# A float32 network of three layers on one core: weight tiles and dense-layer activation tiles at multiples of 64 bytes in SBUF

## The chip, the cores and the metric

The kernel runs on one core of one Trainium2 chip. The metric is the time of the device in microseconds, the median of several executions. A core has five engines with queues of their own: TensorE (PE, with its weight loads shown apart as PEld), VectorE (DVE), ScalarE (ACT), GpSimd (POOL) and SyncE (SP). Its working memory, SBUF, has 128 partitions; an address below is a number of bytes within a partition, the same in all of them.

## The reference

One sequence of 256 tokens with 1024 features goes through a stack of layers in float32. Cut to its frame:

```python
# first block, twice: half-FFN, mixer, half-FFN; the mixers are a sparse attention with
# a short convolution, and then a delta-rule recurrence (RWKV-7) over 16 heads of 64
h = rmsnorm(x, pre_g); h = (silu(h @ w_gate) * (h @ w_up)) @ w_down
x = x + 0.5 * rmsnorm(h, post_g)
x = x + rmsnorm(mixer(rmsnorm(x, g), ...), g_post)
# second block: FFN, a state-space branch beside an attention to the 64 best keys,
# attention to a memory of 256 tokens, FFN; each with layer_norm(ALPHA * x + f(x))
# third block, with 16 tokens in front: FFN, gated linear attention, FFN, FFN,
# windowed attention over shared keys and values, FFN
```

Each FFN has 1024 x 2816 weights for gate and up and 2816 x 1024 for down. Nearly all the arithmetic is in these dense products, `x @ w` for 256 or 272 tokens.

## The kernel before

Activations lie feature-major: a tile [128, k, tokens] holds features on the partitions and tokens along them. Weights are read once from DRAM, in pieces of [128, 1024] float32, 512 KB each. `Mat.load` (L198) starts the DMA into one of six `raw` tiles on SP's queue. `Mat.get` (L216) then parts each piece in two: ScalarE copies it to a float32r tile `wh` (L230), VectorE subtracts that from `raw` and writes the rest to `wl` (L231). There are five tiles of each, used in turn. Activations are parted in the same way into `xh` and `xl` (`split_x`, L254: L263 on ScalarE, L264 on VectorE), `hh` and `hl`, and so on.

A dense product is then three float32r matmuls that add up in PSUM, in `mm3p` (L531):

```python
        t.matmul(out, wh, xh, start=first, stop=False, **kw)    # L534
        t.matmul(out, wh, xl, start=False, stop=False, **kw)    # L535
        t.matmul(out, wl, xh, start=False, stop=last, **kw)     # L536
```

The first operand is stationary: 128 columns of weights, loaded into the array for each matmul. The second moves: 256 or 272 columns of tokens, 1024 or 1088 bytes of a partition. In `proj_tok_steps` (L458 to L460) it is the other way round: weights move, activations are stationary.

The program is one long list of such products with the norms, softmaxes and recurrences between them. A planner doesn't exist; the order of each engine is the order in which the Python emits instructions. `ffn` (L462) does, for each of 11 blocks of 256 columns, all products of gate and of up, and then `out_proj` (L555) the down projection, 22 parts of the contraction for each of four pairs of output tiles. In the mixers, `stagger` and `weave` alternate steps of attention or recurrence with steps of dense products.

Where tiles lie. SBUF is allotted in the order in which pools and tiles are asked for, each tile rounded up to a multiple of 32 bytes. From the left: small constants, `vec` at 16512, `zero`, the table `tab_all` at 18944 (`tables`, L826, through `load_tables`: the arrays `ident`, `ones`, `inv_d` and `causal` side by side, one transfer), and then `raw`, `wh`, `wl`, `x`, `tmp`, `tiny`; from 136480 on the pools of each phase. `tab_all` has 128 + 1 + 128 + 384 = 641 columns, 2564 bytes, rounded to 2592. In the built program that leads to these starts:

| tiles | start | mod 64 |
|---|---|---|
| raw (6), wh (5), wl (5), step 4096 | 21536, 46112, 66592 | 32 |
| x (2), o, tmp's tiles | 87072, 104480, 113184 | 32 |
| hh, hl of the FFN (rows of 1024 or 1088) | 136480, 159008 or 160416 | 32 |
| xh/xl of the FFN, allotted from the right end | 212960 to 228320, step 1024; 211936 to 228256, step 1088 | 32 |
| xh/xl, oh/ol, ysl, yal, mh/ml of the mixers | 136480 and on | 32 |
| mh/ml of the recurrent layer, first place | 137760, 145952 | 32 |
| mh/ml of the recurrent layer, second place | 193152, 201344 | 0 |
| xh/xl of the gated linear attention, step 1088 | 174208 to 190528 | 0 |

A tile's row k starts k times 1024 (or 1088 = 17 x 64) bytes later, and a block of 128 weight columns 512 bytes after the last, so each row and block keeps its tile's offset mod 64.

The names that the change touches: `Rows` (L171), eight tiles [128, n] under one name, used for `xh` and `xl` by `split_x` and for the parts of the memory; `tables` (L826), whose `ones` is a column of ones with which TensorE sums over features (L284), `inv_d` and `ident` the constants of L316 and of transposes; and in `rwkv` (L1114) the small tile `om` (L1138), which follows `tab_rwkv` (258 columns, 1032 bytes, rounded to 1056) and `half` (64 bytes) in the pool `rw`, and is followed by `kn` (128 bytes), `mh`, `ml`, `kf` and `rf`.

Of the kernel before, what the change touches and what calls it, by code (L numbers as in the profile page):

```python
# [24 lines left out]
def weave_steps(gens, width, fill=(), drain=True):  # L25
    """Runs generators a step at a time in turn, `width` of them under way, so that their steps alternate; and one step
    of `fill` for each turn, and what is left of it at last. A generator itself."""
    gens, live, fill = list(gens), [], iter(fill)
    while gens or live:
        next(fill, None)  # L30
        while gens and len(live) < width:
            live.append(gens.pop(0))
        for g in list(live):
            try:
                next(g)
            except StopIteration:
                live.remove(g)
        yield
    if drain:
        yield from fill  # L40
# [7 lines left out]
def stagger(count, a, b, c, fill=(), first=1, each=1, lead=1):  # L48
    """Parts a, b and c of each of `count` pieces of work, b and c `lead` turns after a; `each` steps of `fill` before
    each c and after it, `first` at first."""  # L50
# [15 lines left out]
class Packed:  # L66
    """Columns of one [128, n] array that the host lays out."""
# [21 lines left out]
def slope_vectors(s, slopes):  # L89
    """Columns: 0.125 / slope of each pair's features; -slope [query half, head] of each pair."""  # L90
# [5 lines left out]
class Lazy:  # L96
    """A tile [128, k, n] whose parts are written where they are first asked for."""
# [14 lines left out]
class Net:  # L112
# [30 lines left out]
    def load_tables(self, pool, name, queue=None, **fills):  # L143
        """Arrays [128, width] by name, from one transfer: name=(width, fill)."""
# [16 lines left out]
class Pieces:  # L161
    """A matrix [128, k, columns] in tiles of `each` parts of k."""
# [8 lines left out]
class Rows:  # L171
    """A tile [128, 8, n] that is eight tiles."""

    def __init__(self, p, name, n, dtype=F32R):
        self.t = [p.tile([128, n], dtype, name=f"{name}{k}") for k in range(KD)]
# [5 lines left out]
class Mat:  # L181
# [34 lines left out]
    def get(self, k0, kn, c0, cw, p=128):  # L216
        """Parts of a block of the weights."""
# [18 lines left out]
class Ops(Net):  # L236
    """Norms, splits and dense layers on feature-major activations [128, k, tokens]."""
# [16 lines left out]
    def split_x(self, p, x, n, g=None):  # L254
        """Parts of g * x for products."""
# [22 lines left out]
    def tok_sum(self, parts, n):  # L278
        """Sums over features of [128, n] tiles, tokens on partitions: [128, nt] in PSUM."""
# [9 lines left out]
    def rsqrt(self, v, nt, name="rs"):  # L289
        """v ** -0.5 on a small tile (v positive), by Newton's steps."""  # L290
# [19 lines left out]
    def bcast(self, r, n):  # L310
        """[128, nt] with tokens on partitions to [128, n] in PSUM, the same on all partitions."""
# [8 lines left out]
    def inv_sqrt(self, ss, nt, scale, eps, gain=1.0):  # L320
        """gain * (ss * scale + eps) ** -0.5 on a small tile; eps is a number or a tile. Also the sum under the root."""
# [16 lines left out]
    def hold_weights(self, after=2):  # L338
        """Keeps the parting of the piece of weights that comes after so many from here behind the last inverse root."""
        self.hold, self.held = self.roots, after  # L340

    def warm(self, f, after):
        """The table for the function f, fetched once `after` is there."""
# [6 lines left out]
    def add_to(self, total, t, n):  # L350
        """Adds a [128, n] tile, by GpSimd."""
# [11 lines left out]
    def rms(self, x, n, eps=1e-6):  # L363
        """1 / rms of x's tokens: [128, nt] by tokens and [128, n] on all partitions; eps * (mean squares + eps)."""
# [14 lines left out]
    def norm(self, x, n, eps=1e-6):  # L379
        """rms(x, n), emitted where it is first asked for."""  # L380
# [10 lines left out]
    def proj(self, w, c0, tiles, xh, xl, n, evac):  # L391
        """x @ w, features on partitions, from column c0; evac(first tile, psum [128, m, n])."""
# [21 lines left out]
    def proj_steps(self, w, c0, tiles, xh, xl, n, evac, every=2):  # L414
        """proj for an even number of tiles, in steps of `every` parts of the contraction for two tiles (one if
        n > 256)."""
# [22 lines left out]
    def proj_tok_steps(self, w, c0, cw, xh, xl, n, evac):  # L439
        """x @ w, tokens on partitions, columns c0 to c0 + cw (at most 512); evac(token tile, psum [128, cw]). In steps."""  # L440
# [21 lines left out]
    def ffn(self, x, n, g, wg, wu, wd, out, first=None, side=None, stats=None):  # L462
        """Raw down projection of silu(.) * up; eps / rstd(x) ** 2. `side` is work that follows, in the places of x's
        parts, which it gives back, and gets the norms
        of `stats` tokens of x."""
# [85 lines left out]
    def out_proj_early(self, w, hh, hl, n, chunks, ks):  # L551
        """The first ks parts of the contraction of the first chunks of out_proj, for 8 parts."""
        return EarlyProj(self, w, hh, hl, n, chunks, ks)

    def out_proj(self, w, hh, hl, n, ks, out, early=None, side=None):  # L555
        """h @ w to model features; out.evac(first tile, psum [128, m, n]). `side` prepares work that follows."""
# [29 lines left out]
    def rms_out(self, n):  # L586
        """Takes a projection, to be normed and added to the residual."""
        return RmsOut(self, n)

    def ln_out(self, x, n, alpha, half, close=False):  # L590
        """Takes a projection, to be normed with alpha times the residual."""
        return LnOut(self, x, n, alpha, half, close)

# [5 lines left out]
    def alibi_scores(self, pw, q, k, base, neg, slopes, gate=None):  # L599
        """Weights of causal attention over 256 tokens for two heads: [queries, (k0 of q0: 2 heads, k0 k1 of q1: 2 heads)].  # L600
        q [2 heads' features, queries], scaled by scale / slope; k [2 heads' features, head, keys], zero but for the head;
        neg -slope and gate [128, query half, head]."""
# [24 lines left out]
    def alibi_turn(self, pw, u):  # L627
        """Those weights by keys: [keys, head, (q0 of k0, q1 of k0, q1 of k1)]."""
# [9 lines left out]
    def alibi_values(self, po, t, v, first, last):  # L638
        """Sums of the values v(key half, head) [keys, 64] with those weights: [2 heads' features, queries]."""
# [5 lines left out]
    def rsqrt_full(self, v, y, ps, floor, eps):  # L645
        """y = max(ps, floor) ** -0.5 or (ps + eps) ** -0.5, for a PSUM tile; v is scratch."""
# [51 lines left out]
class RmsOut:  # L698
    """A projection's output o and the sums of its squares; then x + half * rmsnorm(rt * o, g)."""
# [38 lines left out]
class LnOut:  # L738
    """v = alpha * x + half * projection less a value near its mean; then layer norm. The value is the mean of the
    features 0 to 767: what is left of the mean can't exceed the deviations much. `close` if the parts of the projection  # L740
    come close to each other: TensorE then sums more of them."""
# [13 lines left out]
    def square(self, k, m, apart):  # L755
        """Squares of m tiles; summed by GpSimd, or apart."""
# [69 lines left out]
def tables(s):  # L826
    s.load_tables(s.const, "all", s.nc.sync, ident=(128, lambda I: np.eye(128)), ones=(1, lambda I: 1.0),
                  inv_d=(128, lambda I: 1.0 / D), causal=(384, causal_table))
# [35 lines left out]
def nsa(s, x):  # L864
# [4 lines left out]
    with s.phase("nsa") as p, s.phase("nsaw", 2) as pw:  # L869
# [11 lines left out]
        # keys of both branches, zero but for one head  # L881
# [35 lines left out]
        # a pair of heads of one causal branch at a time, all pairs of a branch after another  # L917
# [29 lines left out]
def nsa_compressed(s, p, pw, w, w1, xh, xl, q, gt, rb, vc, pcT):  # L947
    """The compressed branch, in steps: its values and weights."""
# [40 lines left out]
    # slots of 32 partitions: (pair parity, group); columns: pair parity, group, 64  # L989
# [5 lines left out]
    # scores and weights, all heads at once: [query, pair, query half, head of the pair, block]  # L995
# [37 lines left out]
def nsa_conv(s, p, pw, w, xh, xl, rb, oh, ol):  # L1033
    """Gated short convolution, in steps."""
# [63 lines left out]
class Twos:  # L1098
    """A tile [128, 8, 256] that is four tiles, each allotted at its first use."""
# [14 lines left out]
def rwkv(s, x, side):  # L1114
# [15 lines left out]
    with s.phase("rw") as p:  # L1130
# [7 lines left out]
        om = p.tile([128, 8], F32, name="om")  # L1138
        nc.vector.tensor_scalar(om, s.vec_t[:, s.rw["k_a"]:s.rw["k_a"] + 8], -1.0, 1.0, op0=OP.mult, op1=OP.add)
        kn = p.tile([128, 2, 8, 2], F32, name="kn")  # L1140
        with s.phase("rwx") as px:
# [7 lines left out]
            def mix(i):  # L1149
                # the second place outlasts this phase: the values' mix is the last  # L1150
# [53 lines left out]
            # the outputs' parts take the places of keys and receptances  # L1204
# [1328 lines left out]
```

## Time and profile before

| what | before |
|---|---|
| median of 3 runs (lowest, highest) | 3190.02 us (3177.36, 3194.52) |
| span of the profiled execution, first to last instruction | 3186.4 us |
| instructions | 63288 |
| TensorE busy | 3077.6 us, 97% |
| VectorE, ScalarE, GpSimd busy | 65%, 48%, 10% |
| mean granted clock of TensorE | 0.977 |
| DMA | 494.73 MB, mean 155 GB/s |

The profiled execution's own time is its span, 3186.4 us, and a little around it that the page doesn't list; the median of the runs is 3.6 us longer than the span. Busy times of TensorE are those of pipelined matmuls whose ends are modelled, so the time that one costs is read from the starts. The views used below are the page's shares and chain, the groups of instructions by form, tables of stretches of time, and the timeline of TensorE, in which each row is a start in us from the span's begin, a duration, and the instruction.

### The profile page before, as it was taken

Reading aid. Unit: us, or ns where it says so; the run is one execution under the profiler, and the core shown is the slowest. Engines: PE = TensorE matmul, PEld = TensorE weight load, DVE = VectorE, ACT = ScalarE, POOL = GpSimd, SP = SyncE. Lnnn points to the kernel's source line nnn. Section 1 sums busy time; section 2 is a strip of 40 time slices with the busy share of each in tenths; the row PEclk is TensorE's granted clock in tenths of the full one; section 3 lists DMA queues with packets and bytes.
Section 4 is the critical chain, followed back from the end, with each engine's and each line's share of the span. In section 5 each row is a group of like instructions: output and inputs, shape, how many; then the busy total and the mean of one; then the engine's idle time right before and its main releaser. Section 6 shows DMA issues by size and latency. Waiting matters only on the chain.

```text
span 3186.4 us, 63288 instructions
## 1 busy us (share of the span) xinstructions
PE 3077.6 (97%) x26242; PEld 2969.1 (93%) x26242; DVE 2059.9 (65%) x3466; ACT 1526.0 (48%) x2413; POOL 332.6 (10%) x386
## 2 busy tenths in 40 slices
PE   8999999999899999999999999999999999999998
PEld 8998999999878899999989999999979999998898
DVE  6567665657867665657886655566566656658664
ACT  5455544444532544545465454454344444444543
POOL 0010101002222100001100100110112001012101
PEclk9999999999999999999999999999999999999999
DMA  6553565655310355654334536545433555552453
GB/s 239 182 185 124 164 190 179 200 191 160 115 42 29 113 193 195 201 189 160 127 130 153 169 110 199 172 147 175 149 126 106 172 166 166 187 187 87 134 185 112
DMA packets 142528, 494.73 MB, mean 155 GB/s; under 512 B 15760, under 2 KB 18448, under 8 KB 141984
## 3 DMA queue, kind: packets, MB, share of 16 engines
q1 hardware_dynamic: 136512, 478.94, 46.1%
q10 hardware_dynamic: 5696, 11.68, 1.1%
q8 instruction: 205, 3.36, 0.4%
q14 instruction: 83, 0.68, 0.1%
q0 software_dynamic: 32, 0.07, 0.0%
HBM read 487.48 MB, written 3.15 MB: 154 GB/s over the span
## 4 chain that ended last, share of the span: by engine, by line
PE 90%; DVE 5%; POOL 2%; ACT 2%; issue 1%; DMA 0%; SPq 0%; POOLq 0%; DVEq 0%; ACTq 0%
PE acc L534 25%; PE acc L535 25%; PE acc L536 25%; PE aux L1365 2%; DVE wl L231 1%; PE aux L284 1%; PE aux L316 1%; POOL acc L354 1%; PE acc L2368 1%; PE acc L458 1%; PE acc L459 1%; PE acc L460 1%; ACT wh L230 1%; PE aux L1385 0%; DVE t L732 0%
## 5 line engine op out<-in xcount | busy, mean ns | idle before, releaser
L231 DVE TENSOR_TENSOR wl<-raw,wh 128x1024 fp32r<-128x1024 f32 (+2 forms) x934 | 1124.8, 1208 | 746.5 <-ACT wh L230 740.7
L230 ACT CAST wh<-raw 128x1024 fp32r<-128x1024 f32 (+2 forms) x934 | 950.6, 1021 | 1160.5 <-PE acc L535 864.0
L534 PE MATMUL acc<-xh,wh 128*128 128x256 f32 (+1 forms) x4464 | 1268.8, 286 | 28.2 <-ACT xh L263 16.3
L535 PE MATMUL acc<-xl,wh 128*128 128x256 f32 (+1 forms) x4464 | 1263.0, 283 | 1.1 <-DVE xl L264 1.0
L536 PE MATMUL acc<-xh,wl 128*128 128x256 f32 (+1 forms) x4464 | 1261.9, 283 | 0.8 <-DVE wl L231 0.8
L534 PEld LDWEIGHTS acc<-xh,wh 128*128 128x128 f32 x4464 | 850.0, 191 | 36.1 <-ACT xh L263 17.7
L535 PEld LDWEIGHTS acc<-xl,wh 128*128 128x128 f32 x4464 | 851.0, 191 | 6.2 <-issue 3.6
L536 PEld LDWEIGHTS acc<-xh,wl 128*128 128x128 f32 x4464 | 850.5, 191 | 3.3 <-DVE wl L231 1.4
L535 PE MATMUL acc<-hl,wh 128*128 128x256 f32 (+1 forms) x1760 | 501.2, 285 | 0.0
L536 PE MATMUL acc<-hh,wl 128*128 128x256 f32 (+1 forms) x1760 | 501.0, 285 | 0.0
L534 PE MATMUL acc<-hh,wh 128*128 128x256 f32 (+1 forms) x1760 | 501.0, 285 | 0.0
L535 PEld LDWEIGHTS acc<-hl,wh 128*128 128x128 f32 x1760 | 337.4, 192 | 0.1
L534 PEld LDWEIGHTS acc<-hh,wh 128*128 128x128 f32 x1760 | 337.2, 192 | 0.0
L536 PEld LDWEIGHTS acc<-hh,wl 128*128 128x128 f32 x1760 | 337.1, 192 | 0.1
L354 POOL TENSOR_TENSOR acc<-so 128x256 f32<-128x256 f32 (+1 forms) x16 | 19.6, 1225 | 1148.7 <-ACT so L717 1148.1
L354 POOL TENSOR_TENSOR acc<-acc,so 128x256 f32<-128x256 f32 (+1 forms) x68 | 79.0, 1162 | 324.6 <-ACT so L717 321.7
L547 DVE TENSOR_TENSOR gv<-acc,glu 128x512 f32<-128x512 f32 (+1 forms) x130 | 78.0, 610 | 51.0 <-PE acc L536 47.9
L542 DVE TENSOR_TENSOR glu<-acc,rb 128x512 f32<-128x512 f32 (+1 forms) x106 | 61.9, 596 | 39.0 <-PE acc L536 39.0
L534 PE MATMUL acc<-mh,wh 128*128 128x256 f32 x280 | 82.2, 296 | 2.3 <-ACT mh L246 1.5
L535 PE MATMUL acc<-ml,wh 128*128 128x256 f32 x280 | 81.0, 291 | 0.8 <-DVE ml L247 0.7
L536 PE MATMUL acc<-mh,wl 128*128 128x256 f32 x280 | 80.7, 290 | 0.0
L549 DVE TENSOR_TENSOR hl<-gv,hh 128x512 fp32r<-128x512 f32 (+1 forms) x132 | 77.5, 601 | 0.0
(603 smaller groups left out, 3793.9 us busy)
## 6 DMA issues: line engine op xcount, KB each, us to landing
raw<-w SPq DMA_DIRECT2D x880, 512.0 KB, 3.6
raw<-w SPq DMA_DIRECT2D x46, 256.0 KB, 3.1
so<-memT ACTq DMA_DIRECT2D x20, 256.0 KB, 3.7
raw<-w SPq DMA_DIRECT2D x8, 192.0 KB, 3.4
x<-xT SPq DMA_DIRECT2D x4, 256.0 KB, 5.3
mk<-so ACTq DMA_DIRECT2D x4, 256.0 KB, 2.5
mv<-so ACTq DMA_DIRECT2D x4, 256.0 KB, 2.9
mk<-mk ACTq DMA_DIRECT2D x1, 1024.0 KB, 4.7
```

What stands on the lines that cost most here:

```text
L230: nc.scalar.copy(h, r)
L231: nc.vector.tensor_sub(l, r, h.bitcast(F32))
L284: self.nc.tensor.matmul(ps[:, j:j + 1], a[:, j * 128:(j + 1) * 128], self.tab["ones"], start=(j == 0 and i == 0), stop=(j == nt - 1 and i ...
L316: self.nc.tensor.matmul(ps[:, j * 128:j * 128 + w], r[:w, j:j + 1].to_broadcast([w, 128]), self.tab["ident"][:w, :w], start=(j == 0), stop ...
L354: self.nc.gpsimd.tensor_add(d, total[1], t)
L534: t.matmul(out, wh, xh, start=first, stop=False, **kw)
L535: t.matmul(out, wh, xl, start=False, stop=False, **kw)
L536: t.matmul(out, wl, xh, start=False, stop=last, **kw)
L542: nc.vector.tensor_mul(s, pg, rb[:, None, :].to_broadcast([128, m, n]))
L547: nc.vector.tensor_mul(v, pu, s)
L549: nc.vector.tensor_sub(hl, v, hh.bitcast(F32))
L1365: nc.tensor.matmul(ps[R[a], c], lhsT(c, a), rhs(c, a), start=first and c == 0, stop=c == 3, skip_group_check=True)
```

## The change

The table gets the column `ones` last and 16 columns wide, of which the first is used: 656 columns, 2624 bytes, a multiple of 64. `Rows` asks for tiles at multiples of 64 bytes. `om` is allotted 16 columns wide and used as 8. All docstrings and comments are blanked, line by line, which leaves the instructions as they are (one added line in `tables` moves the numbers after it by one).

```diff
 class Rows:
...
-        self.t = [p.tile([128, n], dtype, name=f"{name}{k}") for k in range(KD)]
+        self.t = [p.tile([128, n], dtype, name=f"{name}{k}", align_bytes=64) for k in range(KD)]
...
 def tables(s):
-    s.load_tables(s.const, "all", s.nc.sync, ident=(128, lambda I: np.eye(128)), ones=(1, lambda I: 1.0),
-                  inv_d=(128, lambda I: 1.0 / D), causal=(384, causal_table))
+    s.load_tables(s.const, "all", s.nc.sync, ident=(128, lambda I: np.eye(128)),
+                  inv_d=(128, lambda I: 1.0 / D), causal=(384, causal_table), ones=(16, lambda I: 1.0))
+    s.tab["ones"] = s.tab["ones"][:, :1]
...
-        om = p.tile([128, 8], F32, name="om")
+        om = p.tile([128, 16], F32, name="om")[:, :8]
```

## Rows read from the trace of the kernel before

**Rows 1.** The page: busy time, share of the span and count of each engine; the chain that ended last, by engine and by line.

```profile
PE 3077.6 (97%) x26242; PEld 2969.1 (93%) x26242; DVE 2059.9 (65%) x3466; ACT 1526.0 (48%) x2413; POOL 332.6 (10%) x386
...
PE 90%; DVE 5%; POOL 2%; ACT 2%; issue 1%; DMA 0%; SPq 0%; POOLq 0%; DVEq 0%; ACTq 0%
PE acc L534 25%; PE acc L535 25%; PE acc L536 25%; PE aux L1365 2%; DVE wl L231 1%; PE aux L284 1%; PE aux L316 1%; POOL acc L354 1%; PE acc L2368 1%; PE acc L458 1%; PE acc L459 1%; PE acc L460 1%; ACT wh L230 1%; PE aux L1385 0%; DVE t L732 0%
```

**Rows 2.** Groups of TensorE's instructions by form: line, operation, tiles (out<-moving and stationary), rows * columns of the array, partitions x columns, count | busy us, mean ns of one | idle time before. The groups of L535 and L536 have the same counts as L534.

```profile
L534 PE MATMUL acc<-xh,wh 128*128 128x256 f32 x3656 | 1035.7, 284 | 22.3 <-ACT xh L263 10.4 <-ACT wh L230 7.0 <-ACT xh L246 4.9
...
L534 PE MATMUL acc<-hh,wh 128*128 128x256 f32 x1408 | 399.7, 284 | 0.0
...
L534 PE MATMUL acc<-xh,wh 128*128 128x272 f32 x808 | 233.2, 292 | 5.9 <-ACT xh L263 5.9
...
L534 PE MATMUL acc<-hh,wh 128*128 128x272 f32 x352 | 101.3, 288 | 0.0
L534 PE MATMUL acc<-mh,wh 128*128 128x256 f32 x280 | 82.2, 296 | 2.3 <-ACT mh L246 1.5 <-ACT mh L1613 0.8
...
L534 PE MATMUL acc<-oh,wh 128*128 128x256 f32 x192 | 55.9, 291 | 0.0
```

**Rows 3.** Stretches of time (us from the span's begin): length, and busy us (count) of PE, PEld, DVE, ACT and POOL; then the granted clock, the share of the DMA engines and GB/s. In order: up projections of the second FFN and of the first, a down projection, dense products of the hybrid layer's mixer, up projections with 272 columns, dense products of the recurrent layer with mh/ml of the first place.

```profile
360.00:460.00 100.00, 100.00 (x883) 99.95 (x882) 66.34 (x76) 51.76 (x64) 1.80 (x2) 1.00 0.63 191
40.00:120.00 80.00, 80.00 (x682) 80.00 (x681) 48.51 (x50) 37.08 (x43) 0.00 (x0) 1.00 0.56 185
480.00:520.00 40.00, 40.00 (x336) 40.00 (x335) 21.39 (x26) 18.21 (x26) 4.16 (x3) 1.00 0.61 193
1485.00:1515.00 30.00, 30.00 (x252) 30.00 (x251) 26.36 (x50) 20.60 (x27) 0.43 (x4) 1.00 0.51 173
2120.00:2220.00 100.00, 100.00 (x802) 100.00 (x801) 60.54 (x85) 46.39 (x68) 0.00 (x0) 1.00 0.54 173
780.00:800.00 20.00, 20.00 (x169) 20.00 (x169) 19.02 (x36) 14.43 (x26) 0.00 (x0) 1.00 0.62 203
```

**Rows 4.** Timeline of TensorE in the first three of these stretches: the first and the last of 53, of 51 and of 51 rows that follow one another, all of L534 to L536 in turn.

```profile
399.75 0.28 PE L536 MATMUL acc<-xh,wl 128*128 128x256 f32 x1
...
405.64 0.28 PE L534 MATMUL acc<-xh,wh 128*128 128x256 f32 x1
...
79.82 0.28 PE L536 MATMUL acc<-xh,wl 128*128 128x256 f32 x1
...
85.71 0.28 PE L535 MATMUL acc<-xl,wh 128*128 128x256 f32 x1
...
499.82 0.28 PE L534 MATMUL acc<-hh,wh 128*128 128x256 f32 x1
...
505.82 0.28 PE L536 MATMUL acc<-hh,wl 128*128 128x256 f32 x1
```

**Rows 5.** Timeline of TensorE in up projections with 272 columns: the first, some further and the last of 25 rows that follow one another.

```profile
2150.79 0.28 PE L534 MATMUL acc<-xh,wh 128*128 128x272 f32 x1
2150.91 0.30 PE L535 MATMUL acc<-xl,wh 128*128 128x272 f32 x1
2151.04 0.29 PE L536 MATMUL acc<-xh,wl 128*128 128x272 f32 x1
...
2153.79 0.28 PE L534 MATMUL acc<-xh,wh 128*128 128x272 f32 x1
```

**Rows 6.** At the begin of the gated linear attention: a stretch as in rows 3, and the first and last start of 16 matmuls of 272 columns that follow one another in it.

```profile
2300.20:2304.60 4.40, 4.40 (x20) 4.40 (x21) 4.40 (x12) 3.15 (x9) 2.76 (x3) 0.50 0.00 0
...
2300.78 0.43 PE L535 MATMUL acc<-xl,wh 128*128 128x272 f32 x1
...
2304.18 0.43 PE L535 MATMUL acc<-xl,wh 128*128 128x272 f32 x1
```

**Rows 7.** From the chain that ended last, in order of time (start us, us, what): plain float32 matmuls of 256 columns, which the hardware runs in two passes each, 8 passes in the row.

```profile
859.59 1.73 PE aux L1385 x8
```

**Rows 8.** Timeline of TensorE where the operands' offsets mod 64 differ: mh/ml of the recurrent layer's second place (first and last of 27 rows), xh/xl of the gated linear attention (27 rows), weights as the moving operand over xh/xl of that layer, 512 columns (6 rows).

```profile
805.26 0.28 PE L535 MATMUL acc<-ml,wh 128*128 128x256 f32 x1
...
808.38 0.28 PE L534 MATMUL acc<-mh,wh 128*128 128x256 f32 x1
...
2396.98 0.29 PE L536 MATMUL acc<-xh,wl 128*128 128x272 f32 x1
...
2400.24 0.28 PE L535 MATMUL acc<-xl,wh 128*128 128x272 f32 x1
...
2340.22 0.40 PE L458 MATMUL acc<-wh,xh 128*16 128x512 f32 x1
...
2341.38 0.39 PE L460 MATMUL acc<-wh,xl 128*16 128x512 f32 x1
```

**Rows 9.** What TensorE waited for (us in total, times, longest), the first; and the two groups of products that read the table, as in rows 2.

```profile
PE aux L316 <- DVE isc L334: 17.9, 14, 2.2
...
L284 PE MATMUL aux<-tab_all,acc 128*128 128x1 f32 x180 | 24.2, 243 | 7.7 <-POOL acc L354 6.7 <-ACT acc L714 0.5
L316 PE MATMUL aux<-tab_all,isc 128*128 128x128 f32 x112 | 21.6, 321 | 18.0 <-DVE isc L334 17.9
```

**Rows 10.** ScalarE's splitting of x with 272 columns, as in rows 2: from 2290 to 2330 us, where its target lies at 0 mod 64, and from 2070 to 2110 us, where it lies at 32.

```profile
L263 ACT ACTIVATE xh<-x,vec 128x272 fp32r<-128x272 f32 x8 | 3.9, 517 | 6.7 <-DVE x L733 6.7
...
L263 ACT ACTIVATE xh<-x,vec 128x272 fp32r<-128x272 f32 x8 | 3.7, 508 | 0.0
```

## The prediction

> **What bounds the kernel now.** I read the shares of the engines and the chain that ended last first: TensorE is busy 97% of the 3186.4 us, and three lines of one helper, the dense products L534 to L536, make 75% of the chain [rows 1]. So a nanosecond on each dense matmul is a nanosecond of the whole, wherever TensorE doesn't wait. Then the groups by form, to count them: 3 x (3656 + 1408) products of 256 columns and 3 x (808 + 352) of 272 columns in the dense layers with Rows and hh/hl parts, 3 x 192 with oh/ol and 3 x 280 with mh/ml [rows 2]. The duration printed there (about 284 ns) is no cost: matmuls overlap. The cost is the pitch, from one start to the next, and it is read from a table by stage and from the timeline.
>
> The stages don't run at one pitch. At a granted clock of 1.00, the 2.4 GHz level, 100 us of one up projection hold 883 matmuls, 80 us of another, with operands at the same addresses, hold 682, and 40 us of a down projection 336 [rows 3]. From the starts: 5.89 us over 52 steps are 113.3 ns, 5.89 us over 50 steps 117.8 ns, 6.00 us over 50 steps 120.0 ns [rows 4]. The mixers' dense products run like the last: 252 in 30 us in the hybrid layer, 169 in 20 us in the recurrent one [rows 3]. In cycles of 2.4 GHz that is 272, 282.7 and 288 for 256 columns. The products of 272 columns take 3.00 us over 24 steps, 125.0 ns or 300 cycles, though single steps lie between 120 and 130 ns, in a pattern that comes back [rows 5]. None of it is a wait: TensorE shows no idle time in these stretches, and in those of the FFNs DVE is busy 53 to 66% and the DMA engines 54 to 63% [rows 3]. So each product pays 16 to 32 cycles above its columns.
>
> Two rows say what kind of cost that is. Where the granted clock is 0.50 (1.2 GHz), 272 columns take 3.40 us over 15 steps, 226.7 ns, which is 272 cycles with nothing on top [rows 6]. And a plain float32 product of 256 columns, which feeds its columns at half the rate, takes 1.73 / 8 = 0.216 us, 519 cycles for 2 x 256, 7 on top [rows 7]. The surcharge is there only where columns of 4 bytes are wanted at the full rate. 272 = 17 x 16 and 288 = 18 x 16: it comes in steps of 16 columns, which are 64 bytes of a partition. A row of 256 columns that starts 32 bytes past a multiple of 64 touches 17 pieces of 64 bytes, one of 272 columns 18, against 16 and 17 from a multiple of 64. My reading: the moving operand comes in pieces of 64 bytes, one per 16 cycles at best, and the weights' pieces now and then cost it one more.
>
> **The change part by part.** (1) The table is 15 columns wider: 7.5 KB of 494.73 MB in one early load, 0.05 us at the mean 155 GB/s of the table of times, beside the weights' own loads. No instruction is added or removed, no queue or wait changes. (2) From the table on, the left side moves by 32 bytes: raw, wh, wl, x, tmp, hh/hl, oh/ol, q, yal and the rest go from 32 to 0 mod 64; Rows tiles, on the right side too, by their request. Nothing else moves against the others in the stages named above, so moving operand and weights are then both on multiples of 64.
>
> The price of (2) is not in the trace: no float32r product has both operands there. It has three near cases with one. The mh/ml of the recurrent layer's second place lie at 0, the weights at 32: 3.12 us over 26 steps, 120.0 ns. The xh/xl of the linear-attention layer lie at 0, its weights at 32: 3.26 us over 26 steps, 125.4 ns. With weights moving (at 32) over xh as stationary (at 0), 512 columns take 1.16 us over 5 steps, 232 ns, 45 cycles on top [rows 8]. So one aligned operand gains nothing. I take this to mean that two streams half a piece apart meet more often: the piece saved by the one is lost again. Both ends for a product with both aligned: at best the columns and the 7 cycles of rows 7, about 109.6 ns and 116.3 ns; at worst 120.0 ns for all of 256 columns, the highest steady pitch in rows 4 and 8, and 125.4 for 272. I take one piece (16 cycles, 6.67 ns) less than now for each product, since the pieces of a row fall by one and the relation of the streams stays.
>
> Sum: 3 x (3656 + 1408 + 808 + 352 + 192) = 19,248 products x 6.67 ns = 128 us. Of 3 x 280 with mh/ml, 3 x 64 are the merge's and gain 1 us more; the recurrent layer's 648 I leave out: tab_rwkv, half and om before mh sum to 1056 + 64 + 32 bytes and kn adds 128, together 1280, a multiple of 64; with om twice as wide they sum to 1312, and mh/ml and kf/rf stay at 32 while the weights go to 0. With mixed offsets rows 8 show 120.0 ns, and mh/ml at 32 over weights at 32 run 169 in 20 us, some 119 [rows 3]: no cost, no gain beyond 1 us. So 129 us.
>
> What hides nothing: TensorE's own idle time is 3186.4 - 3077.6 = 109 us, waits for the norms and mixers' chains [rows 1, 9], and stays. When the dense stages run 5% faster, DVE goes from 66% to about 70% of an FFN's stretch, the DMAs from 63 to about 66%, and in the hybrid mixer DVE from 26.36 of 30 us, 88%, to some 93% [rows 3]: cover remains, least in the mixers. (3) The table's parts move: inv_d and causal from 4 past to a multiple of 64, so L316 and L284, 112 + 180 products [rows 9], could each gain or lose a piece, under 2 us. (4) ScalarE and DVE write the tiles at other places: L263 takes 517 ns in the layer where its target is at 0 and 508 ns where it is at 32 [rows 10]; either is off the chain.
>
> A rule of the Trainium skill speaks against the change. The page "SBUF — State Buffer", Specifications (TRN2), gives lines of 16 bytes and full bandwidth as long as a line is hit at least twice. By that rule a start at 32 mod 64 begins on a line already, as one at 0 does, and the sum would be 0. It doesn't explain why pitches of rows 4 differ by 16 columns, but neither do these rows refute it; it stands beside the first rival. Another, "TensorE: Matmul & The Clock Gate", section "Wait — 56ns, not 53.3ns?", has warm matmuls at N / 2.4 plus about 2.5 ns, which is 109.2 ns for 256 columns; rows 4 lie 4 to 11 ns over it, and by it the sum would be near the best end below.
>
> The profiled span is 3186.4 us, the median of the three runs 3190.0; some 3.6 us lie around the span. Forecast: 3186.4 - 129 + 3.6 = 3061, as **3060 us**.
>
> **The rivals.** (a) No change. What counts is how the two streams lie to one another, and that isn't touched: hh/hl and wh/wl move by the same 32 bytes. For it: the same addresses give 113.3 and 117.8 ns in rows 4, so the state is a matter of phase; and one aligned operand gains nothing in rows 8. Against it: steps of exactly 16 columns. Time: 3190. (b) Half the gain: the piece saved stays hidden in a floor of 272 cycles, and only the extra ones go, so that all stages run like the best. Up projections of 256 columns have a mean near 116 ns (between 113.3 and 117.8, with the mixers' at 120): 10,968 x 2.7 = 30 us; hh/hl, 4,224 x 6.7 = 28; 272 columns at 120, 3,480 x 5 = 17; oh and mh, 1,416 x 6.7 = 9. 84 us, 3106. (c) Slower: the phase locks the wrong way. The up projections' xh/xl are allotted from the right end, and their place against wh/wl can shift by 64 bytes; it is the one kind of stage that reaches 113.3. Should it lock as hh/hl do, at 120.0, 10,968 products lose 4 ns each: 44 us, 3234. This decides once the first up projections after 40 us show 120 in the timeline. (d) The best end: all of the surcharge but 7 cycles goes: 10,968 x 6.4 + 4,224 x 10.4 + 3,480 x 8.7 + 1,416 x 10.4 = 159 us, 3031. That the change doesn't do what it says holds for the recurrent layer's tiles alone, priced above.
>
> **How the numbers follow.** About 0.5%, 16 us, is what a measurement tells from no change. Forecast with (d) 0.42, (a) 0.34, (b) 0.12, (c) 0.12. Faster 0.54, same 0.34, slower 0.12. The range is 3010 to 3205: the low end is 20 us under (d), for the small groups that aren't in rows 2, the high end holds (a) and its spread and leaves (c) out. The forecast's own range is 3020 to 3095.
>
> **What would show it.** Right: pitches of 106 to 113 ns in the dense stages of 256 columns and 116 to 120 at 272, all stages alike, the recurrent layer's mh/ml unchanged, counts and order of instructions unchanged. If the up projections still show 113 and 118 and the down projections 120.0, (a) holds and the reading in pieces is wrong. If 272 columns fall below 120 but 256 stay at 113.3, (b). If TensorE shows idle time before L534 behind ACT wh L230 or DVE wl L231, the weights' splitting has become late and the gain is cut there. A pitch that falls while the span does not would be a gain off the path, which rows 1 speak against.

## The result, and the profile after

The changed kernel takes 3203.36 us in the median of 20 runs, the kernel before on the same chip 3183.16 us: a ratio of 1.0055 [1.0041, 1.0069], about 0.5% slower, where 3060 us had been forecast; it lies inside the stated range only by luck, since the upper end of 3205 was set for the rival without change and the rival of a slower kernel was left out of it. One run of 7587.52 us, disturbed, is left out of the ratio. The profiled execution has a span of 3206.8 us, 20.4 us more than before, for the same 63288 instructions.

The page of the changed kernel: shares and counts of the engines.

```profile
PE 3096.0 (97%) x26242; PEld 2988.0 (93%) x26242; DVE 2059.7 (64%) x3466; ACT 1525.7 (48%) x2413; POOL 331.3 (10%) x386
```

Beside [rows 1]: TensorE is busy 18.4 us longer, and the other engines as long as before; TensorE's idle time is 110.8 us, where it was 108.8. So no new wait of that size has come; TensorE does the same work more slowly. Where, a table of stretches shows. Its columns are those of [rows 3] cut to TensorE: stretch and length in us, busy us and count of matmuls, granted clock, DMA share, GB/s. Matmuls of 0.28 us that only overlap an edge count too, some 2.4 for each stretch, so the pitch is the length over the count less 2.4. First the kernel before, in up projections of five FFNs:

```profile
60.00:120.00 60.00, 60.00 (x512) 1.00 0.55 185
...
580.00:640.00 60.00, 60.00 (x511) 1.00 0.62 186
1100.00:1190.00 90.00, 90.00 (x796) 1.00 0.60 194
1290.00:1370.00 80.00, 80.00 (x708) 1.00 0.63 203
...
1910.00:1990.00 80.00, 80.00 (x709) 1.00 0.61 199
```

The changed kernel, the same stretches, the stretch of 100 us of [rows 3] and, at 485 us, a down projection:

```profile
60.00:120.00 60.00, 60.00 (x512) 1.00 0.61 185
360.00:460.00 100.00, 100.00 (x852) 1.00 0.62 186
485.00:525.00 40.00, 40.00 (x336) 1.00 0.62 197
580.00:640.00 60.00, 60.00 (x512) 1.00 0.63 190
1100.00:1190.00 90.00, 90.00 (x766) 1.00 0.60 188
1290.00:1370.00 80.00, 80.00 (x682) 1.00 0.64 201
...
1910.00:1990.00 80.00, 80.00 (x682) 1.00 0.59 187
```

Two things are to be seen. The four up projections that ran at 113.2 to 113.6 ns (883 in [rows 3], 796, 708, 709) now run at 117.7 (852, 766, 682, 682); those that ran at 117.7 (512, 511) are where they were. And the down projection, whose operands both went from 32 to 0 mod 64, holds 336 as in [rows 3]: 120.0 ns, not a cycle better. Four stages of 1056 products lose 4.1 to 4.5 ns each: 18 us of the 20.4. Another 2.9 us lie in the linear attention, where a stretch of the same 323 matmuls got a granted clock of 0.92, not 1.00; I put that to the run and not to the change: a kernel below that is faster than both, the one with every row at place 192, shows the same dip (45.3 us at 0.92), and the changed kernel's own runs differ, with mean granted clocks from 0.975, that of the profiled execution, to 0.981. Before, then after:

```profile
2377.80:2420.30 42.50, 42.46 (x323) 1.00 0.31 100
```

```profile
2394.10:2439.50 45.40, 45.40 (x323) 0.92 0.29 93
```

Why the up projections fell stands in the addresses of the built programs. With `align_bytes=64` the eight tiles of a `Rows` no longer lie 1024 bytes apart: `xh` of the FFN starts at 212480, 213504, 214592, 215616, 216704 and on, steps of 1024 and 1088 in turn. The starts of weight tiles are equal mod 256, and blocks within them step by 512. So against the weights, mod 256, all rows stood at 192 before; now two rows stand at 192, two at 0, two at 64, two at 128. I call this distance, mod 256, a row's place. Each row of `xh` and `xl` is used by six products that follow one another, so two rows make 12. The timeline of the changed kernel in the up projection at 400 us walks through all four places (start us, us, instruction; the first and last line of stretches of 7, 6, 11 and 10):

```profile
400.31 0.28 PE L536 MATMUL acc<-xh,wl 128*128 128x256 f32 x1
...
400.99 0.28 PE L536 MATMUL acc<-xh,wl 128*128 128x256 f32 x1
...
401.81 0.28 PE L534 MATMUL acc<-xh,wh 128*128 128x256 f32 x1
...
402.40 0.28 PE L536 MATMUL acc<-xh,wl 128*128 128x256 f32 x1
...
402.64 0.28 PE L535 MATMUL acc<-xl,wh 128*128 128x256 f32 x1
...
403.82 0.28 PE L536 MATMUL acc<-xh,wl 128*128 128x256 f32 x1
403.94 0.28 PE L534 MATMUL acc<-xh,wh 128*128 128x256 f32 x1
...
405.00 0.28 PE L534 MATMUL acc<-xh,wh 128*128 128x256 f32 x1
```

The first pair of lines lies at place 192: 0.68 us over 6 steps, 113 ns. The second is at 0: 0.59 over 5, 118 ns, and from 402.04 on single steps of 120. The third is at 64: 1.18 over 10, 118 ns. The fourth is at 128: 1.06 over 9, 118 ns, made of uneven steps of 0.11 to 0.13 us. The first products after a change of place still run unevenly: over the whole stage the first of the two rows at 192 has a mean step of 117.5 ns, the second 113.3. That is a reading of one trace; the experiments test it.

The kernel before had such a stage too, which the prediction overlooked: the up projection at 2670 us works on 256 tokens in tiles made for 272, so its rows step by 1088 bytes, stand at 192, 0, 64 and 128 in turn, and run at 117.0 ns (80 us over 683.6):

```profile
2700.00:2780.00 80.00, 80.00 (x686) 1.00 0.58 188
```

### The profile page after: what moved, and what is told of

It is laid out like the page before. It is cut to its first block, busy times and chain, and to the rows that moved or that the text cites. A ratio compares the mean times of both kernels' runs of the same rounds, so it can differ in the third digit from the quotient of the medians.

```text
span 3206.8 us, 63288 instructions
## 1 busy us (share of the span) xinstructions
PE 3096.0 (97%) x26242; PEld 2988.0 (93%) x26242; DVE 2059.7 (64%) x3466; ACT 1525.7 (48%) x2413; POOL 331.3 (10%) x386
## 4 chain that ended last, share of the span: by engine, by line
PE 90%; DVE 6%; ACT 2%; POOL 2%; issue 1%; DMA 0%; SPq 0%; POOLq 0%; DVEq 0%; ACTq 0%
PE acc L534 26%; PE acc L535 25%; PE acc L536 25%; PE aux L1366 2%; DVE wl L231 1%; PE aux L284 1%; PE aux L316 1%; POOL acc L354 1%; PE acc L2369 1%; ACT wh L230 1%; PE acc L458 1%; PE acc L459 1%; PE acc L460 1%; PE aux L1386 0%; PE aux L606 0%
## 5 line engine op out<-in xcount | busy, mean ns | idle before, releaser
L534 PE MATMUL acc<-xh,wh 128*128 128x256 f32 (+1 forms) x4464 | 1276.1, 287 | 28.6 <-ACT xh L263 16.9
L535 PE MATMUL acc<-xl,wh 128*128 128x256 f32 (+1 forms) x4464 | 1268.5, 285 | 1.1 <-DVE xl L264 1.1
L536 PE MATMUL acc<-xh,wl 128*128 128x256 f32 (+1 forms) x4464 | 1266.7, 284 | 0.7 <-DVE wl L231 0.7
L534 PEld LDWEIGHTS acc<-xh,wh 128*128 128x128 f32 x4464 | 850.7, 191 | 36.4 <-ACT xh L263 18.3
L535 PEld LDWEIGHTS acc<-xl,wh 128*128 128x128 f32 x4464 | 851.6, 191 | 6.3 <-issue 3.6
L536 PEld LDWEIGHTS acc<-xh,wl 128*128 128x128 f32 x4464 | 851.3, 191 | 2.9 <-issue 1.3
L535 PE MATMUL acc<-hl,wh 128*128 128x256 f32 (+1 forms) x1760 | 500.7, 284 | 0.0
L534 PE MATMUL acc<-hh,wh 128*128 128x256 f32 (+1 forms) x1760 | 500.2, 284 | 0.0
L536 PE MATMUL acc<-hh,wl 128*128 128x256 f32 (+1 forms) x1760 | 499.9, 284 | 0.0
L536 PEld LDWEIGHTS acc<-hh,wl 128*128 128x128 f32 x1760 | 337.0, 191 | 0.1
L535 PEld LDWEIGHTS acc<-hl,wh 128*128 128x128 f32 x1760 | 336.9, 191 | 0.1
L534 PEld LDWEIGHTS acc<-hh,wh 128*128 128x128 f32 x1760 | 336.9, 191 | 0.0
L534 PE MATMUL acc<-mh,wh 128*128 128x256 f32 x280 | 81.8, 294 | 2.2 <-ACT mh L246 1.4
L535 PE MATMUL acc<-ml,wh 128*128 128x256 f32 x280 | 80.7, 290 | 1.1 <-DVE ml L247 1.1
L536 PE MATMUL acc<-mh,wl 128*128 128x256 f32 x280 | 80.1, 288 | 0.0
```

## The experiments

Three theories stand against one another. P is the prediction's: pieces of 64 bytes, alignment pays. R: what counts is a row's place against the weights mod 256. L: 113.3 ns was luck, and any move of the tiles loses it. The median of the kernel before is given anew for each experiment, from runs on the same chip; where the ratio is missing, there was one run.

**Aligned, with even steps.** The change's table, no request in `Rows`, and 224 free bytes behind the FFN's `xl`, so that rows and weights lie at 0 mod 64 and rows keep place 192. Against the changed kernel:

```diff
-            self.t = [p.tile([128, n], dtype, name=f"{name}{k}", align_bytes=64) for k in range(KD)]
+            self.t = [p.tile([128, n], dtype, name=f"{name}{k}") for k in range(KD)]
...
             xh, xl = self.split_x(px, x, n, g)
+            px.tile([128, 56], F32, name="tail")
```

> The table of the changed kernel, but Rows without its request, and 224 bytes left free at the right end of the FFN's pool: all of raw, wh, wl, xh/xl and hh/hl of the FFN lie at multiples of 64, the rows of xh/xl step by an even 1024 again, and xh/xl stand to wh/wl as in the kernel before (192 bytes past, mod 256). Theory P (the prediction's pieces of 64 bytes: alignment pays as long as rows and weights are both on it): up projections below 113.3 ns, some 3060 to 3110 us. Theory R (what counts is where a row stands against the weights, mod 256, and the uneven step of the changed kernel breaks that): up projections of the second FFN and those near 1100 us back at 113.3 to 114 ns, down projections at 120.0, time as before within 0.2% (ratio 0.998 to 1.002). Theory L (any move of the tiles loses a lucky state): up projections at 117.7 ns, ratio about 1.0055 as in the changed kernel.

Measured: 3178.64 us to 3186.22 before, ratio 0.9982 [0.9963, 1.0001]. Its stretches:

```profile
360.00:460.00 100.00, 100.00 (x883) 1.00 0.68 195
485.00:525.00 40.00, 40.00 (x336) 1.00 0.69 218
580.00:640.00 60.00, 60.00 (x532) 1.00 0.68 194
1100.00:1190.00 90.00, 90.00 (x797) 1.00 0.62 191
...
1910.00:1990.00 80.00, 80.00 (x709) 1.00 0.65 193
```

883, 336, 797 and 709 are the counts of the kernel before. The up projection at 580 us is not the same: 532 in 60 us, 113.3 ns, where the kernel before holds 511 at the same place. So place 192 doesn't fix the pitch by itself; more on that below. It isn't the alignment's doing, since a kernel below with everything at 32 mod 64 holds 532 there as well. Down projections with both operands on multiples of 64 gain nothing (P falls), and a move of everything loses nothing as long as the places stay (L falls as it was put). The two kernels also tell 256 from 512: mod 512 these rows stood at 448 before and stand at 192 here.

**Uneven steps, nothing aligned.** The kernel before, with the steps of the changed one.

```diff
-        self.t = [p.tile([128, n], dtype, name=f"{name}{k}") for k in range(KD)]
+        self.t = []
+        for k in range(KD):
+            self.t.append(p.tile([128, n], dtype, name=f"{name}{k}"))
+            if k % 2:
+                p.tile([128, 16], dtype, name=f"{name}gap{k}")
```

> The kernel before, with 64 bytes left free after every second row of xh and xl: the rows step by 1024 and 1088 in turn as in the changed kernel, but everything stays at 32 mod 64. Theory P: no change of the pitch, ratio 1.000. Theory R: the up projections that ran at 113.3 to 113.7 ns go to 117.7 ns, four stages of some 1056 products each, about +18 us and a little back in the mixers' products (119.7 to 117.5 ns): ratio 1.004 to 1.007. Theory L: the same as R here.

Measured: 3203.67 us, ratio 1.0064 [1.0037, 1.0091], the changed kernel's loss, without its alignment.

```profile
360.00:460.00 100.00, 100.00 (x852) 1.00 0.63 185
...
1100.00:1190.00 90.00, 90.00 (x767) 1.00 0.61 191
```

The counts are the changed kernel's to within one. Steps that spread the rows over four places are enough for the whole slowdown.

**The places swapped.** If R holds, the down projections can be given the place of the up projections, and the other way round.

```diff
-    def split_x(self, p, x, n, g=None):
+    def split_x(self, p, x, n, g=None, lead=48):
...
+        if lead:
+            p.tile([128, lead], F32, name="lead")
         xh, xl = Rows(p, "xh", n), Rows(p, "xl", n)
...
-            xh, xl = self.split_x(px, x, n, g)
+            xh, xl = self.split_x(px, x, n, g, 0)
+            px.tile([128, 48], F32, name="tail")
+            p.tile([128, 48], F32, name="lead")
             hh = p.tile([128, FF // 128, n], F32R, name="hh")
```

> The kernel before with xh/xl of the FFN moved down by 192 bytes, and hh/hl and the mixers' xh/xl up by 192, even steps, nothing aligned: against the weights, mod 256, the FFN's xh/xl now stand at 0 (where hh/hl stood) and hh/hl and the mixers' at 192 (where the FFN's xh/xl stood). Theory R: the pitches swap: up projections 120.0 ns, down projections 113.3 to 118 ns; 8448 up products by up to +4.5 ns and 4224 down products by -2 to -6.7 ns, together between 3180 and 3215 us. Theory P: pitches as before (113.3 to 118 up, 120.0 down). Theory L: up 117.7, down 120.0.

Measured: 3189.13 us in one run, beside 3186.22.

```profile
360.00:460.00 100.00, 100.00 (x835) 1.00 0.63 186
485.00:525.00 40.00, 40.00 (x355) 1.00 0.66 217
...
2120.00:2200.00 80.00, 80.00 (x642) 1.00 0.56 174
```

They swap: up 835 in 100 us, 120.1 ns; down 355 in 40 us, 113.4 ns. The last row is an up projection of 272 columns: 80 / 639.6 = 125.1 ns, as in [rows 5]. That doesn't show that products of this width are free of the place: their rows step by 1088 bytes, so a stage passes through four places whichever one it starts at, and only the mean stays. Sorted by place, from the starts in the trace and the addresses in the program, with some 800 products of 272 columns at each, the steps of the kernel before have means of 123.8 ns at 192, 125.7 at 0, 125.1 at 64 and 126.2 at 128; in the swapped kernel they are 123.6, 124.7, 125.5 and 126.3. So 192 is the best of the four at this width too, by 1 to 3 ns.

**Other places.** The same edit with 64, 128 and 160 bytes (and 224 at the right end in the last).

> As the kernel with 192 bytes, but by 64: the FFN's xh/xl stand 128 past the weights, hh/hl and the mixers' 64. A look at two further places. Theory R: pitches other than 113.3 and 120.0, the same over the whole of a stage; near 118 by what the rows at 64 and 128 show in the changed kernel (118.1 to 118.5 ns). Theory P: as before. Theory L: up 117.7, down 120.0.

> A further look: hh/hl and the mixers' xh/xl moved up by 128 (128 past the weights), the FFN's xh/xl down by 128 (64 past). Theory R: down projections near 118.7 ns, as the up projections at 128 with the 64-byte shift, and up projections near 117.8 as the down projections at 64 there. Theory P and L: down projections 120.0.

> A look at places that are odd multiples of 32 from the weights: hh/hl and the mixers' xh/xl moved up by 160 (160 past the weights and at 0 mod 64, the weights at 32), the FFN's xh/xl down by 224 (224 past, at 0 mod 64). Theory R: pitches between those of the neighbours: down between 113.4 (at 192) and 118.7 (at 128), up between 113.4 (at 192) and 120.0 (at 0). Theory P: mixed offsets, 118 to 120 in both.

They took 3191.32, 3196.93 and 3198.37 us in one run each. By 64 (up at place 128, down at 64; the third row has the hybrid mixer's products, at 64 too), by 128 (up 64, down 128), by 160 (up 224, two down projections at 160):

```profile
360.00:460.00 100.00, 100.00 (x845) 1.00 0.64 186
485.00:525.00 40.00, 40.00 (x342) 1.00 0.67 212
1485.00:1515.00 30.00, 30.00 (x267) 1.00 0.51 159
```

```profile
360.00:460.00 100.00, 100.00 (x851) 1.00 0.62 189
485.00:525.00 40.00, 40.00 (x339) 1.00 0.68 216
```

```profile
360.00:460.00 100.00, 100.00 (x847) 1.00 0.61 187
485.00:525.00 40.00, 40.00 (x343) 1.00 0.69 211
680.00:720.00 40.00, 40.00 (x340) 1.00 0.65 203
```

Read as pitches, the two kinds of stage agree at each place that both have had, though their loops differ:

| place of the row, mod 256 | 0 | 64 | 128 | 160 | 192 | 224 |
|---|---|---|---|---|---|---|
| up projections, ns | 120.1 | 117.8 | 118.7 | 117.5 or 118.5 | 113.6 or 117.7 | 118.4 |
| down projections, ns | 119.9 | 117.8 | 118.8 | 117.4 or 118.5 | 113.4 or 117.8 | |

(The up projections' two values at 160 are from the next kernel, the down projections' 117.8 at 192 from the one after.) What was expected of 64 and 128 came out in these stages; "between the neighbours" at 160 and 224 held too, but says little. One thing was not expected: the hybrid mixer's products at place 64 ran at 113.4 ns (267 in 30 us), where the FFN's at 64 took 117.8. So 113 ns is not 192's alone, and three places, 64, 160 and 192, were seen with two pitches each. A modulus of 128 would not do: 0 and 128 differ, 120.0 and 118.7.

**The table without the request.** Part of the change alone: the FFN's rows keep their addresses while the weights move by 32, which puts them at place 160; down projections keep place 0. Against the changed kernel:

```diff
-        self.t = [p.tile([128, n], dtype, name=f"{name}{k}", align_bytes=64) for k in range(KD)]
+        self.t = [p.tile([128, n], dtype, name=f"{name}{k}") for k in range(KD)]
```

> The change without the request of Rows: table of 656 columns and the wider om, so that raw, wh, wl, hh/hl and the mixers' rows go to 0 mod 64, the FFN's xh/xl stay at 32 and stand 160 past the weights mod 256; all steps even. Theory P: one operand aligned in the up projections (no gain there), both in the down projections (113.3 for 120.0, 28 us): ratio 0.99. Theory R: down projections unchanged at 120.0; up projections at another place of theirs, 113 to 120 ns, the same over the stage: ratio 0.996 to 1.008. Theory L: 1.0055.

Measured: 3206.35 us, ratio 1.0075 [1.006, 1.009].

```profile
60.00:120.00 60.00, 60.00 (x513) 1.00 0.59 186
360.00:460.00 100.00, 100.00 (x846) 1.00 0.60 182
485.00:525.00 40.00, 40.00 (x335) 1.00 0.62 201
```

The up projections run at 117.5 or 118.5 ns, the down projections at 120.0 as ever. So the table and `om` alone already cost what the whole change costs (the intervals, 1.006 to 1.009 and 1.0041 to 1.0069, overlap), by moving the weights 32 bytes under the rows. Dropping the request mends nothing; giving the rows back their place, as in the first experiment, does.

**Every row at place 192.** The kernel before, with the up projections left alone and 192 bytes ahead of `hh` and of the mixers' `xh`; the recurrent layer's `mh` and `ml` stay at 0, and rows that step by 1088 at their four places. `split_x` is that of the swapped kernel, and in `ffn`:

```diff
-            xh, xl = self.split_x(px, x, n, g)
+            xh, xl = self.split_x(px, x, n, g, 0)
+            p.tile([128, 48], F32, name="lead")
             hh = p.tile([128, FF // 128, n], F32R, name="hh")
```

> The kernel before with 192 bytes left free ahead of hh and ahead of the mixers' xh/xl, the FFN's xh/xl where they were: everything stands 192 past the weights mod 256, at 32 mod 64, with even steps. Theory R: down projections of 256 columns at 113.4 ns as with the 192-byte shift (eight of them, 63.2 to 59.7 us, 28 us), mixers' products at 114.9 to 117.8 ns for 119.5 to 119.9 (4 to 10 us), up projections as before: 3183 - 32 to 38 = 3145 to 3155 us, ratio 0.988 to 0.991. Theory P: 1.000. Theory L: 1.000 to 1.006, each move loses something.

Measured: 3159.03 us to 3181.49, ratio 0.9923 [0.9899, 0.9947]: faster, by less than expected.

```profile
360.00:460.00 100.00, 100.00 (x851) 1.00 0.64 189
485.00:525.00 40.00, 40.00 (x342) 1.00 0.72 218
680.00:720.00 40.00, 40.00 (x355) 1.00 0.73 232
```

The down projection at 680 us runs at 113.4 ns, the one at 485 at 117.8, at the same addresses; and the up projection at 360, untouched by the edit, fell from 883 to 851. Place 192 has two pitches, and here a stage that wasn't moved took the other one; that much of theory L stays. Whether the moves elsewhere did it or this execution, one trace can't tell. Two more kernels: one with the recurrent layer's `mh`/`ml` at 192 as well, one that does all of this with the change's table (and so with 224 bytes behind the FFN's `xl`, and 160 here), so that weights and rows lie at 0 mod 64:

```diff
         om = p.tile([128, 8], F32, name="om")
+        p.tile([128, 48], F32, name="lead")
```

> The kernel with everything 192 past the weights, and 192 bytes more ahead of kn, so that the recurrent layer's mh/ml of the first place stand 192 past them too (they stood at 0, 120 ns). Everything at 32 mod 64. Theory R: these go to 113.3 or 117.8 ns, 1 to 5 us; down projections of 256 columns at 113.3 or 117.8, never at 120.0; which of the two a stage takes may differ from the run before (two of its stages of up and two of down projections were at 117.5 and 117.8): 3135 to 3165 us, ratio 0.985 to 0.994.

> The same places against the weights (192 mod 256) and even steps, but with the table of the changed kernel: weights, xh/xl, hh/hl and mh/ml of the first place all at 0 mod 64. Theory P in its weaker form (alignment to 64 bytes is worth something beside the place): pitches under 113.3 ns, faster than the kernel with 192 at 32 mod 64 by over 0.5%. Theory R: the same as that kernel within 0.4%, ratio 0.985 to 0.994, and no pitch under 113.3.

Measured: 3162.67 us, ratio 0.9905 [0.9871, 0.994], and 3157.15 us, ratio 0.9895 [0.9865, 0.9924], to 3188.99. The first, with 10 us of the recurrent layer's products at the end, and the second:

```profile
360.00:460.00 100.00, 100.00 (x882) 1.00 0.65 196
485.00:525.00 40.00, 40.00 (x356) 1.00 0.71 226
762.00:772.00 10.00, 10.00 (x88) 1.00 0.49 156
```

```profile
360.00:460.00 100.00, 100.00 (x851) 1.00 0.62 189
485.00:525.00 40.00, 40.00 (x342) 1.00 0.70 224
```

Alignment adds nothing that the intervals could tell. These three kernels beat the kernel before by 0.8 to 1.1%, and with it the changed one; which of them is best isn't settled, since their runs spread over 3138 to 3174 us.

## Why the prediction was wrong

**What bounds the kernel.** Right. TensorE's pitch is the time; each run moved as its counts did, while in all kernels DVE and ACT were busy as long as before within 3 us and TensorE idle for 109 to 115 us.

**Step (2), the price.** This failed, in the sentence "I take one piece (16 cycles, 6.67 ns) less than now for each product, since the pieces of a row fall by one and the relation of the streams stays". The pieces bring nothing: down projections stayed at 120.0 ns with both operands at 0 mod 64, in the changed kernel and in the first experiment, so the 128 us of the sum are 0. Pitches 16 cycles apart were real, but they go with the place: a steady 120.0 stood at 0, 113.3 at 192 (and once at 64), and other places gave 117.4 to 118.8 in between, where a reading in pieces has no room. The 300 cycles of 272 columns, no multiple of 16 either, are a mean over four places; that is the pattern that comes back in [rows 5].

**Step (2), what moves.** This failed too, in "Nothing else moves against the others in the stages named above". It holds for `hh` and `hl`. The FFN's `xh` and `xl` did move, by the request's uneven steps and by the weights' 32 bytes; the table of starts had only the kernel before, and the starts of `Rows` in the changed kernel were not worked out. The cost of this is the 18 us.

**The rivals.** (a) had the mechanism ("how the two streams lie to one another"), and the down projections are unchanged as it says; for the up projections it held that this relation isn't touched, and it was. (c) had the mechanism and the place of the loss: up projections lose the 113.3. It was too large: it priced 10,968 products at 4 ns, to 120.0, 44 us; only four stages were at 113.3 to begin with, and they went to a mix of places at 117.7, so 4 x 1056 products lost 4.1 to 4.5 ns. Its chance of 0.12 was too small, given [rows 4], where the one kind of stage with another place was also the one that reached 113.3.

**The one-aligned cases** of [rows 8] were taken as a sign that both operands must be aligned. They couldn't tell alignment from place: `mh`/`ml` of the second place stand 96 past the weights, and the linear attention's rows at 96, 160, 224 and 32 in turn.

**Steps (1), (3) and (4).** The table's load is invisible. L316 went from 21.6 us in [rows 9] to 20.9 for its 112 products and L284 from 24.2 to 24.1 for its 180, within the bound of 2 us.

ACT and DVE are busy as long as before, in all 1525.7 and 2059.7 us. The recurrent layer's `mh`/`ml` of the first place stayed at 32 mod 64, as the prediction said; but their place against the weights went from 0 to 32, and with it their pitch from 120.0 ns (169 in 20 us in [rows 3]) to 117.9 (both stretches hold some 25 to 30 products of the second place as well):

```profile
780.00:800.00 20.00, 20.00 (x172) 1.00 0.59 174
```

That is some 2 ns for each of 432 products, about the 1 us that the prediction allowed at most, but not for its reason. At place 192 they did 88 in 10 us, 116.8 ns. The hybrid mixer's rows, which the request spread over four places as well, gained too: 258 in 30 us for 252.

**The two rules beside the rivals.** Lines of 16 bytes, from the Trainium skill, "SBUF — State Buffer", Specifications (TRN2), gave a sum of 0 for the alignment, and the first experiment agrees: 0.9982. The other rule, from the Trainium skill, "TensorE: Matmul & The Clock Gate", section "Wait — 56ns, not 53.3ns?", gives an estimate of 109.2 ns for 256 columns. It was reached at no place: the lowest steady pitch seen is 113.3 ns, and here the measurement decides.

## What to carry to other kernels

Before an allocation is changed, list the start of every operand in both builds and compare the distance of the moving rows to the stationary tiles, row by row; an alignment request may change the step between tiles as well as their start. Where TensorE has hardly any idle time, as here, the pitch of equal products in different stages is worth more attention than the waits: 120 against 113 ns was 6%, and free bytes in front of a tile were enough to move a stage from one to the other. A place that one stage has by chance can be given to the others, and it has to be measured again after any change of the layout.

## What the runs showed that was not expected

The pitch depends on the distance between the streams modulo 256 bytes, and up and down projections, whose loops differ, agree at each of the four places at multiples of 64. Products of 272 columns show a smaller dependence, row by row, that the mean of a stage hides. What in the hardware makes the distance count was not tested and stays open.

Place 192 has two pitches, 113.3 and 117.8 ns, and so have 64 (113.4 and 117.8) and 160 (117.4 and 118.5). The same up projection at 360 us, at the same place, held 883, 883, 851, 882 and 851 matmuls in 100 us in five kernels. In one place of the traces the pitch changes right where another kind of product comes between. In the kernel with every row at 192 (its L537 to L539 are the dense products, its L318 the broadcast of the norm):

```profile
536.80 0.28 PE L537 MATMUL acc<-xh,wh 128*128 128x256 f32 x1
...
537.86 0.28 PE L537 MATMUL acc<-xh,wh 128*128 128x256 f32 x1
537.98 0.61 PE L318 MATMUL aux<-tab_all,isc 128*128 128x128 f32 x4
...
538.55 0.28 PE L539 MATMUL acc<-xh,wl 128*128 128x256 f32 x1
...
540.02 0.28 PE L537 MATMUL acc<-xh,wh 128*128 128x256 f32 x1
```

Before the four float32 records, 1.06 us over 9 steps, 117.8 ns; behind them 1.47 over 13, 113.1 ns. What decides which pitch comes out was not tried, and so it stays open whether the best kernels could be held at 113.3 throughout.

The spread of the runs has two parts. One goes with the clock: the changed kernel's runs stand in groups near 3197, 3203 and 3209 us, with mean granted clocks of 0.979, 0.977 and 0.975. The other is left at an equal clock. At 0.977 six runs of the changed kernel lie between 3202.96 and 3204.54 us, and five of the kernel before, on the chip of the first experiment, between 3178.22 and 3192.95. The changed kernel has no stage wholly at place 192, and all its up projections ran near 117.7 ns, so the two pitches of that place, 4 to 5 us for an up projection, are a likely source of the second part; but only one execution of each kernel was profiled, so it is not shown.
